# Attention's block products as chains, and PSUM banks of three kinds

## The chip, the cores and the metric

The kernel runs on one core of a Trainium2 chip. Its engines are TensorE (PE, with its weight loads shown as PEld), VectorE (DVE), ScalarE (ACT), GpSimd (POOL) and SyncE (SP), which issues most transfers. PE writes its results to PSUM, which has eight banks; one bank holds 512 float32 values in each of 128 partitions. DVE and ACT read and write PSUM too. The metric is the device time of one execution in microseconds, the median of several runs.

## What is computed

A decoder trunk of two layers on 512 positions with 1024 channels, float32 throughout. Layer 0 mixes by attention, layer 1 by causal pooling; a SwiGLU FFN of width 2816 follows each, every sub-layer starts with an RMS norm, and a last norm ends the trunk.

```python
for i in range(DEPTH):
    if i % 2 == 0:
        x = x + dilated_attention_mixer(rmsnorm(x, attn_norm[j]), w_qkv[j], w_attn_out[j])
    else:
        x = x + pooling_mixer(rmsnorm(x, pool_norm[j]), w_pool_in[j], w_pool_group[j], pool_scale[j])
    x = x + swiglu_ffn(rmsnorm(x, ffn_norm[i]), w_ffn_gate_up[i], w_ffn_down[i])
return rmsnorm(x, final_norm)
```

Attention has three groups of eight heads. In each, a query sees a causal window with a stride (windows 128, 512 and 2048, strides 1, 4 and 16) and a bias that falls with distance; the three outputs of a head slot are merged by their softmax denominators.

## The kernel before, in words

**Products in three passes.** Activations lie with channels on partitions and the 512 positions along the free axis. Each float32 operand is split in a high and a low part (`split`: an ACT copy gives `whi`, a DVE subtraction, L97, gives `wlo`), and each product is three matmuls: high by high, high by low, low by high. A plain product (`Product`, L272 to L275) has 24 matmuls of 512 columns.

**Block products.** Most weight products are done as seven block products instead of eight, in the Winograd form of Strassen's scheme: a 1024x512 piece of weights is a 2 by 2 of blocks, the activations are halves of 256 columns, and the block products are called "11", "21", "1", "3", "2", "22" and "4". Each is `mult` (L389 to L391): up to twelve matmuls of 256 columns into half a bank. The weights come in the parts b, s, m and l, two block products each except the last.

There are two ways to put the seven together before the change:

- `chain` in the FFN. Partial sums stay in PSUM. Four half-width values c, a, d, e each take a bank of their own (tags `sum`, `ps`, `seed`, `seed`). The order is: "11" into c; ACT copies c to d (L463); "1" into a, read by `share`; "2" onto c; ACT copies c to e (L471); "21" onto d, read by `left`; "3" onto c, read by `high`; "22" onto e, read by `right`; "4" onto c, read by `low`. There are 17 gate/up chains in each layer (`strassen_pair`, whose readers are L1065 to L1072: two DVE subtractions, and ACT copies and Silu) and 12 `down` chains in each layer (L1078 to L1087, whose readers are DVE additions to x; `share` has two, L1080 and L1081): 34 and 24.
- `seven` in attention, for q and k of heads 2 to 7 (18 of them) and for v of group 0 (3). It takes four banks, lets PE fill p26, p73 and p45 in both halves, and adds up on DVE (L430, L436 or L438, L443, L444), with one ACT copy at the start (L417). With `blocks` the result is written in another order of positions, by small strided pieces.

`values12` (v of groups 1 and 2, for heads 1, 3, 5 and 7) does its seven block products with the roles of weights and activations exchanged, each into a whole bank.

**Between the products.** After each block product `step` or `behind` is called. It calls `pump`, which issues at most one piece of weight preparation (loads through SP and POOL, splits on ACT and DVE) for products to come, and in attention also some work of other heads: `scores0`, `scores12`, `merge` (whose small matmuls L682 need `far` from DVE, L678), `turn0`, `turn12` (transposes), `output`. That work takes PSUM banks as well.

**Banks.** PSUM tiles are asked for by tag: `ps` 3 banks, `seed` 3, `sum` 2. Until the end of attention, a request without a tag goes through all eight in a fixed ring; later, products without a chain alternate between `ps` and `seed` (`full`), and everything else takes `ps`.

**What sets the order.** The source is traced from top to bottom, without loops at run time. The framework then fixes the order of each engine's instructions at compile time: it goes through them by an estimate of their durations, and each engine gets the earliest instruction in the source that is expected to be ready. Where the next one is expected to wait, a later one is put ahead of it. On the chip that order no longer changes. The framework places the waits too: an instruction waits for those before it in the source, on other engines, that touch the same data; in PSUM it keeps accesses of different engines to one bank in source order, whichever columns they touch. A tile's bank is handed to a new tile once all readers of the old one are done.

**PSUM sums.** In the program, a matmul with the flag `start` begins its sum anew, and does so for all places of its bank; one without it overwrites a place that hasn't been written since, and adds to one that has.

Of the kernel before, what the change touches and what calls it, by code (L numbers as in the profile page):

```python
# [15 lines left out]
P = 128  # L16
S = 512
# [34 lines left out]
def trunk(ctx: ExitStack, tc: tile.TileContext, xT, norms, w_first, w_qk, w_qkp, w_v0, w_v0p, w_v12, w_out, w_pair, w_down, w_down0, w_down1, w_down2, w_pin, w_pgrp,  # L52
# [15 lines left out]

    turn = {"ring": 0, "full": 0}
# [311 lines left out]
    def in_place(t, a=slice(0, 2)):  # L381
        return t[:, a.start * H2:a.stop * H2]
# [15 lines left out]
    def seven(T, one, two, scratch, after={}, blocks=False):  # L398


        unit, = units.popleft()
        into, left, right = by_block if blocks else in_place, slice(0, 1), slice(1, 2)

        def again(v):
            return v.unsqueeze(1).to_broadcast([P, 2, H2])

        p1, p26, p45, p73 = ps(), ps(), ps(), ps()

        def behind(i):
            pump()  # L410
            for f in after.get(i, ()):
                f()

        w = part(unit, "b")
        mult(p1[:, :H2], w, 0, T, "11")
        first, sums = scratch("first"), scratch("sums")
        nc.scalar.copy(first[:, :H2], p1[:, :H2])  # L417
        behind(0)
        mult(p26[:, :H2], w, 1, T, "21")
        w.done()  # L420
        behind(1)
        w = part(unit, "s")
        mult(p45[:, H2:], w, 0, T, "1")
        behind(2)
        mult(p73[:, :H2], w, 1, T, "3")
        w.done()
        behind(3)
        w = part(unit, "m")
        mult(p26[:, H2:], w, 0, T, "2")
        nc.vector.tensor_add(into(one), p26, again(first[:, :H2]))  # L430
        behind(4)
        mult(p73[:, H2:], w, 1, T, "22")
        w.done()
        if blocks:
            for a in (left, right):
                nc.vector.tensor_add(in_place(sums, a), in_place(p73, a), into(one, right))  # L436
        else:
            nc.vector.tensor_add(sums, p73, again(one[:, H2:]))  # L438
        behind(5)
        w = part(unit, "l")  # L440
        mult(p45[:, :H2], w, 0, T, "4")
        w.done()
        nc.vector.tensor_sub(into(two), p45, again(sums[:, :H2]))  # L443
        mark.append(nc.vector.tensor_sub(into(one, right), sums[:, H2:], p45[:, H2:]))  # L444
        behind(6)

    def chain(T, share, left, right, low, high, behind=None):


        unit, = units.popleft()  # L450
        n = unit.q // P
        c, a, d, e = (ps(tag)[:, :H2] for tag in ("sum", "ps", "seed", "seed"))
        turns = iter(range(7))

        def step():
            pump()
            i = next(turns)
            if behind:
                behind(i)

        wb = part(unit, "b")
        mult(c, wb, 0, T, "11", n=n)
        nc.scalar.copy(d, c)  # L463
# [7 lines left out]
        nc.scalar.copy(e, c)  # L471
# [12 lines left out]
        step()  # L484
        wl = part(unit, "l")
        mult(c, wl, 0, T, "4", True, n=n)
        wl.done()
        low(c)
        step()

    def normed(layer, k, row, h, t, flip=False):

# [7 lines left out]
        nc.vector.tensor_sub(t[:, H2:S], t[:, :H2], h[:, 3 * H2:])  # L500
        if flip:
            nc.vector.scalar_tensor_tensor(t[:, 3 * H2:], t[:, H2:S], -1.0, h[:, S:3 * H2],
                                           op0=OP.mult, op1=OP.subtract)
        else:
            nc.vector.tensor_add(t[:, 3 * H2:], t[:, H2:S], h[:, S:3 * H2])

    def halves_of(hi, lo):
        return [tuple(v[:, a * H2:(a + 1) * H2] for v in (hi, lo)) for a in range(2)]


# [4 lines left out]
    with tc.tile_pool(name="opool", bufs=1) as opool:  # L515
        early = opool.tile([P, HEADS, S], F32R, tag="o", name="early")
        with tc.tile_pool(name="apool", bufs=1) as apool:
# [15 lines left out]
            def values12(after={}):  # L533
# [5 lines left out]
                def product(name, half, key):  # L539
                    p = ps()  # L540
                    for a in range(2):
                        for k in range(K2):
# [3 lines left out]
                            o = both(p)[:, a]  # L546
                            nc.tensor.matmul(o, mh, wh, start=k == 0, stop=False)
                            nc.tensor.matmul(o, mh, wl, start=False, stop=False)
                            nc.tensor.matmul(o, ml, wh, start=False, stop=k == K2 - 1)
                        pump()  # L550
# [306 lines left out]
            for h in range(1, HEADS):  # L857
                for g in range(3):
# [6 lines left out]
                    else:  # L865
                        for c in range(2):
                            QKV[h, g, c] = apool.tile([P, S], F32, name=f"qk{g}{c}")
                        seven(T, QKV[h, g, 0], QKV[h, g, 1], scratch, between(h, g), g == 0)
                if h == 1:
# [8 lines left out]
                if h % 2 == 0:  # L878
                    VT[:] = [apool.tile([P, S], F32, tag=tag, name="vt") for tag in ("row", "o0")]
                    seven(T, *VT, scratch, {0: [later(scores12, h)]}, True)  # L880
                elif h < HEADS - 1:
# [24 lines left out]

            turn["ring"] = None
            for m in range(KC):
# [10 lines left out]
    with tc.tile_pool(name="fpool", bufs=1) as fpool:  # L919
# [16 lines left out]
        def ffn(layer, nxt, lead, row, wk):  # L936
# [98 lines left out]
            def prepare(k):  # L1035


                h, t = wide(("hp", k), "hp"), wide(("tp", k), "tp")
                normed(op, k, row, h, t, True)
                hq, b22 = h.rearrange("p (a b c) -> p a b c", a=2, b=2), h[:, 3 * H2:]  # L1040
# [320 lines left out]
```

## Time and profile before

| what | us |
|---|---|
| median of 3 runs | 1256.29 |
| lowest and highest | 1254.66, 1256.69 |
| the profiled execution, its own time | 1255.83 |
| its span, first to last instruction | 1254.1 |
| attention, first part with plain products | 0 to 100 |
| attention, block products | 100 to 440 |
| end of attention, output product | 440 to 510 |
| FFN of layer 0 | 510 to 854 |
| pooling | 854 to 913 |
| FFN of layer 1 | 913 to 1236 |
| last norm | 1236 to 1254 |

The lower rows are times from the start of the span. In a busy share, PE needs care: matmuls are pipelined, and the recorded length of one (0.28 us at 256 columns) is more than twice the distance to the next (0.12 us). A row of the timeline gives start and length, so the distance of starts shows a stall that a busy share hides. In a row of the waits, the numbers are total time, times and the longest.

### The profile page before, as it was taken

Reading aid. Unit: us, or ns where it says so; the run is one execution under the profiler, and the core shown is the slowest. Engines: PE = TensorE matmul, PEld = TensorE weight load, DVE = VectorE, ACT = ScalarE, POOL = GpSimd, SP = SyncE. Lnnn points to the kernel's source line nnn. Section 1 sums busy time; section 2 is a strip of 40 time slices with the busy share of each in tenths; the row PEclk is TensorE's granted clock in tenths of the full one; section 3 lists DMA queues with packets and bytes.
Section 4 is the critical chain, followed back from the end, with each engine's and each line's share of the span. In section 5 each row is a group of like instructions: output and inputs, shape, how many; then the busy total and the mean of one; then the engine's idle time right before and its main releaser. Section 6 shows DMA issues by size and latency. Waiting matters only on the chain. (4 is left out here: it accounts for less than half of the span.)

```text
span 1254.1 us, 23222 instructions
## 1 busy us (share of the span) xinstructions
PE 1237.9 (99%) x9060; PEld 1172.9 (94%) x9060; DVE 1012.5 (81%) x1687; ACT 680.2 (54%) x1171; POOL 157.4 (13%) x147
## 2 busy tenths in 40 slices
PE   9999999999999999999999999999999999999996
PEld 7889999999999998889999999988789999999996
DVE  7987788878778847798777878798999877888875
ACT  6445554445455544456456557563456646656652
POOL 1011111102111010101111111000310111111100
PEclk9999999999999999999999999999999999999998
DMA  8436566655756444437776786653145777677742
GB/s 292 107 86 173 130 158 142 162 131 156 179 135 152 127 150 132 109 85 187 186 187 165 175 202 169 153 179 118 51 118 124 176 179 183 157 201 189 172 109 68
DMA packets 76719, 189.91 MB, mean 151 GB/s; under 512 B 7600, under 2 KB 15936, under 8 KB 76608
## 3 DMA queue, kind: packets, MB, share of 16 engines
q1 hardware_dynamic: 51120, 141.74, 35.5%
q0 software_dynamic: 24336, 45.63, 22.4%
q8 instruction: 71, 1.16, 0.4%
q10 hardware_dynamic: 1152, 1.05, 0.3%
q14 instruction: 40, 0.33, 0.1%
HBM read 186.29 MB, written 2.10 MB: 150 GB/s over the span
## 5 line engine op out<-in xcount | busy, mean ns | idle before, releaser
L96 ACT ACTIVATE whi<-raw 128x1024 fp32r<-128x1024 f32 (+2 forms) x315 | 318.8, 1016 | 252.6 <-PE seed L390 78.6
L97 DVE TENSOR_TENSOR wlo<-raw,whi 128x1024 fp32r<-128x1024 f32 (+2 forms) x315 | 366.4, 1166 | 107.0 <-ACT whi L96 106.2
L158 POOL DMA_DIRECT2D raw<-w_pair x34 | 41.1, 1209 | 312.0 <-DMA raw<-w_pair 52.6
L389 PE MATMUL sum<-tt,whi 128*128 128x256 f32 x272 | 76.9, 283 | 1.2 <-ACT seed L471 0.8
L390 PE MATMUL sum<-tt,whi 128*128 128x256 f32 x272 | 76.6, 281 | 0.0
L391 PE MATMUL sum<-tt,wlo 128*128 128x256 f32 x272 | 76.4, 281 | 0.0
L96 ACT ACTIVATE halfhi<-rawhalf 128x512 fp32r<-128x512 f32 (+1 forms) x87 | 53.2, 612 | 20.0 <-PE sum L390 12.7
L173 DVE TENSOR_TENSOR raw<-raw 128x512 f32<-128x512 f32 (+1 forms) x87 | 57.5, 661 | 2.5 <-issue 2.4
L174 DVE TENSOR_TENSOR raw<-raw 128x512 f32<-128x512 f32 (+1 forms) x87 | 57.5, 661 | 0.2
L97 DVE TENSOR_TENSOR halflo<-rawhalf,halfhi 128x512 fp32r<-128x512 f32 (+1 forms) x87 | 57.4, 661 | 0.0
L158 POOL DMA_DIRECT2D raw<-w_down x24 | 28.9, 1206 | 214.1 <-DMA raw<-w_down 70.8
L389 PEld LDWEIGHTS sum<-tt,whi 128*128 128x128 f32 x272 | 51.3, 189 | 1.6 <-ACT seed L471 1.0
L471 ACT COPY seed<-sum 128x256 f32<-128x256 f32 x58 | 20.8, 359 | 57.9 <-PE sum L391 57.8
L390 PEld LDWEIGHTS sum<-tt,whi 128*128 128x128 f32 x272 | 51.2, 188 | 0.0
L391 PEld LDWEIGHTS sum<-tt,wlo 128*128 128x128 f32 x272 | 51.2, 188 | 0.0
L389 PE MATMUL sum<-hz,whi 128*128 128x256 f32 x160 | 45.4, 284 | 0.5 <-ACT seed L471 0.3
L390 PE MATMUL sum<-hz,whi 128*128 128x256 f32 x160 | 45.2, 283 | 0.0
L390 PE MATMUL seed<-hy,whi 128*128 128x256 f32 x160 | 45.2, 282 | 0.0
L391 PE MATMUL seed<-hy,wlo 128*128 128x256 f32 x160 | 45.1, 282 | 0.0
L391 PE MATMUL sum<-hz,wlo 128*128 128x256 f32 x160 | 45.1, 282 | 0.0
L389 PE MATMUL seed<-hy,whi 128*128 128x256 f32 x160 | 45.0, 281 | 0.0
L158 POOL DMA_DIRECT2D raw<-w_qkp x18 | 22.0, 1222 | 165.6 <-DMA raw<-w_qkp 100.1
(608 smaller groups left out, 4625.0 us busy)
## 6 DMA issues: line engine op xcount, KB each, us to landing
raw<-w_pair SPq DMA_DIRECT2D x78, 512.0 KB, 4.7
raw<-w_qkp SPq DMA_DIRECT2D x36, 512.0 KB, 4.4
raw<-w_pair POOLq DMA_DIRECT2D x34, 512.0 KB, 7.8
raw<-w_down SPq DMA_DIRECT2D x32, 384.0 KB, 4.2
raw<-w_v SPq DMA_DIRECT2D x18, 512.0 KB, 4.1
raw<-w_qkp POOLq DMA_DIRECT2D x18, 512.0 KB, 7.2
rawhalf<-w_pair SPq DMA_DIRECT2D x34, 256.0 KB, 4.6
raw<-w_down SPq DMA_DIRECT2D x16, 512.0 KB, 4.6
```

Of the source, the lines that this page charges most:

```text
L96: nc.scalar.activation(hi, v, AF.Copy)
L97: nc.vector.tensor_tensor(lo, v, hi.bitcast(F32), op=OP.subtract)
L158: nc.gpsimd.dma_start(b.rearrange("p (a c) -> p a c", a=2), self.src[:, None, 3 * q:].to_broadcast([P, 2, q]), accum_op=OP.add)
L173: nc.vector.tensor_add(a[:, :q], a[:, :q], b[:, :q])
L174: nc.vector.tensor_add(a[:, q:2 * q], a[:, q:2 * q], a[:, :q])
L389: nc.tensor.matmul(dst, w.t[0][:, c], th, start=k == 0 and not onto, stop=False, skip_group_check=onto)
L390: nc.tensor.matmul(dst, w.t[0][:, c], tl, start=False, stop=False, skip_group_check=onto)
L391: nc.tensor.matmul(dst, w.t[1][:, c], th, start=False, stop=k == n - 1, skip_group_check=onto)
L471: nc.scalar.copy(e, c)
```

## The change

The seven block products of attention are done by `chain` as well, and the banks are dealt out anew. `chain` now takes two banks where it took four: c and a are the halves of one `sum` bank, d and e the halves of one `seed` bank. `ps` has four banks, `seed` two, `sum` two; `ps` is for all work other than products, `full` goes through `seed`, `sum`, `ps` in turn, throughout the kernel.

Since two values share a bank, only the first matmul into it carries `start`: "1" goes onto a without it, and in `values12` ("folded values") the second half no longer has a `start` of its own. The idle matmuls at the beginning write both halves of the `seed` banks.

For `chain` to give the signs that attention needs, `normed` always makes the last quarter with the sign that the FFN had, so `low` in `seven` copies with a factor of -1, and the last subtraction of `values12` becomes an operation with the sign turned.

```diff
-RING = ("ps", "seed", "sum", "ps", "seed", "sum", "ps", "seed")
-BANKS = {"ps": 3, "seed": 3, "sum": 2}
+RING = ("seed", "sum", "ps")
+BANKS = {"ps": 4, "seed": 2, "sum": 2}
...
-    def ps(tag=None):
-
-        if tag is None:
-            if turn["ring"] is None:
-                tag = "ps"
-            else:
-                tag = RING[turn["ring"] % len(RING)]
-                turn["ring"] += 1
+    def ps(tag="ps"):
         return psum.tile([P, S], F32, tag=tag, name=tag, bufs=BANKS[tag])
 
     def full():
 
-        if turn["ring"] is not None:
-            return ps()
         turn["full"] += 1
-        return ps(("ps", "seed")[turn["full"] % 2])
+        return ps(RING[turn["full"] % len(RING)])
...
+    def halves_of(*t):
+        parts = [tuple(v[:, a * H2:(a + 1) * H2] for v in t) for a in range(2)]
+        return parts if len(t) > 1 else [v for v, in parts]
...
     def chain(T, share, left, right, low, high, behind=None):
...
-        c, a, d, e = (ps(tag)[:, :H2] for tag in ("sum", "ps", "seed", "seed"))
+        (c, a), (d, e) = (halves_of(ps(tag)) for tag in ("sum", "seed"))
...
         ws = part(unit, "s")
-        mult(a, ws, 0, T, "1", n=n)
+        mult(a, ws, 0, T, "1", True, n=n)
         share(a)
...
+    def seven(T, one, two, half, after={}, blocks=False):
+
+
+        into, left, right = by_block if blocks else in_place, slice(0, 1), slice(1, 2)
+
+        def behind(i):
+            for f in after.get(i, ()):
+                f()
+
+        chain(T, lambda p: nc.scalar.copy(half, p),
+              lambda p: nc.scalar.copy(into(one, left), p),
+              lambda p: mark.append(nc.vector.tensor_sub(into(one, right), p, half)),
+              lambda p: nc.scalar.activation(into(two, left), p, AF.Copy, scale=-1.0),
+              lambda p: nc.vector.tensor_sub(into(two, right), half, p), behind)
...
-    def normed(layer, k, row, h, t, flip=False):
+    def normed(layer, k, row, h, t):
...
                 def product(name, half, key):
-                    p = ps()
+                    p = full()
...
-                            nc.tensor.matmul(o, mh, wh, start=k == 0, stop=False)
+                            nc.tensor.matmul(o, mh, wh, start=k == a == 0, stop=False, skip_group_check=a > 0)
...
-                mark.append(nc.vector.tensor_sub(quarter(0, 1), both(m4), both(u3)))
+                mark.append(nc.vector.scalar_tensor_tensor(quarter(0, 1), both(m4), -1.0, both(u3), op0=OP.mult, op1=OP.subtract))
...
-            spare = ps()
-            for i in range(WARM):
-                nc.tensor.matmul(spare[:, :H2], idle[:, :P], idle, start=True, stop=True)
+            for i in range(WARM // 2):
+                for half, p in enumerate(halves_of(ps("seed"))):
+                    nc.tensor.matmul(p, idle[:, :P], idle, start=half == 0, stop=True, skip_group_check=half > 0)
```

The old `seven`, with its four banks and its sums on DVE, goes.

More of the change, by code (lines that the diff above doesn't have):

```diff
@@ L396, in part @@
         return unit.w[name]
[L398 to L445, printed above, removed]
+    def halves_of(*t):
+        parts = [tuple(v[:, a * H2:(a + 1) * H2] for v in t) for a in range(2)]
+        return parts if len(t) > 1 else [v for v, in parts]
     def chain(T, share, left, right, low, high, behind=None):
@@ L500, in normed @@
         nc.vector.tensor_sub(t[:, H2:S], t[:, :H2], h[:, 3 * H2:])
[L501 to L508, printed above, removed]
+        nc.vector.scalar_tensor_tensor(t[:, 3 * H2:], t[:, H2:S], -1.0, h[:, S:3 * H2], op0=OP.mult, op1=OP.subtract)
     def in_a_row(t):
@@ L546, in product @@
                             o = both(p)[:, a]
[L547 to L549 removed]
+                            nc.tensor.matmul(o, mh, wh, start=k == a == 0, stop=False, skip_group_check=a > 0)
+                            nc.tensor.matmul(o, mh, wl, start=False, stop=False, skip_group_check=a > 0)
+                            nc.tensor.matmul(o, ml, wh, start=False, stop=k == K2 - 1, skip_group_check=a > 0)
                         pump()
@@ L867, in trunk @@
                             QKV[h, g, c] = apool.tile([P, S], F32, name=f"qk{g}{c}")
-                        seven(T, QKV[h, g, 0], QKV[h, g, 1], scratch, between(h, g), g == 0)
+                        seven(T, QKV[h, g, 0], QKV[h, g, 1], scratch("half")[:, :H2], between(h, g), g == 0)
                 if h == 1:
@@ L879, in trunk @@
                     VT[:] = [apool.tile([P, S], F32, tag=tag, name="vt") for tag in ("row", "o0")]
-                    seven(T, *VT, scratch, {0: [later(scores12, h)]}, True)
+                    seven(T, *VT, scratch("half")[:, :H2], {0: [later(scores12, h)]}, True)
                 elif h < HEADS - 1:
@@ L1038, in prepare @@
                 h, t = wide(("hp", k), "hp"), wide(("tp", k), "tp")
-                normed(op, k, row, h, t, True)
+                normed(op, k, row, h, t)
                 hq, b22 = h.rearrange("p (a b c) -> p a b c", a=2, b=2), h[:, 3 * H2:]
```

3 lines of the change are left out of this document (1 added, 2 removed).

## The prediction

> **What bounds the kernel now.** I read the page first, for the engine that is never free:
>
> ```profile
> PE 1237.9 (99%) x9060; PEld 1172.9 (94%) x9060; DVE 1012.5 (81%) x1687; ACT 680.2 (54%) x1171; POOL 157.4 (13%) x147
> ```
>
> PE sets the time, and the change leaves every matmul in place (the six idle ones at the start too). So it can win only where PE stands still, and lose only where it makes PE stand still. Next, by stage (the columns are window, PE, PEld, DVE, ACT, POOL busy, granted clock, DMA share, GB/s): block attention, the first FFN, the end.
>
> ```profile
> 100.00:440.00 340.00, 337.86 (x2818) 336.33 (x2818) 272.88 (x429) 174.41 (x311) 49.44 (x50) 1.00 0.60 150
> ...
> 510.00:854.00 344.00, 341.91 (x2578) 326.72 (x2577) 288.98 (x485) 204.52 (x348) 36.79 (x31) 1.00 0.64 164
> ...
> 1236.00:1254.00 18.00, 8.15 (x52) 7.28 (x51) 9.23 (x26) 2.70 (x7) 2.92 (x4) 0.70 0.36 118
> ```
>
> Block attention has 2.1 us without PE in 340, the first FFN 2.1 in 344. DVE is 80% busy in attention (272.88 of 340) and ACT 51%, but neither is what PE waits for. PE's own waits say what is:
>
> ```profile
> PE ps L682 <- DVE far L678: 2.1, 3, 0.8
> ...
> PE sum L389 <- ACT seed L471: 1.1, 2, 0.8
> PE sum L389 <- ACT seed L463: 0.6, 2, 0.4
> ```
>
> and the waits of all engines show who follows whom:
>
> ```profile
> ACT whi L96 <- PE seed L390: 78.6, 113, 3.4
> ```
>
> Weight splits wait for PE to free a buffer, so weights are ahead of PE. The 58 FFN chains, whose copies are L463 and L471, cost PE 1.7 us in four waits: today's chain is almost free of waits because each of its four values has a bank of its own, and PE writes another bank while ACT or DVE reads.
>
> **What the change takes away.** In attention 21 products (18 for q/k, 3 for v) become chains. Two rows of the DVE groups, and one of ACT:
>
> ```profile
> L430 DVE TENSOR_TENSOR qk<-seed,first 128x512 f32<-128x512 f32 x8 | 5.5, 684 | 0.0
> ...
> L444 DVE TENSOR_TENSOR qk<-sums,sum 128x256 f32<-128x256 f32 x5 | 2.1, 412 | 0.0
> ```
>
> ```profile
> L96 ACT ACTIVATE whi<-raw 128x1024 fp32r<-128x1024 f32 x83 | 87.6, 1059 | 112.7 <-PE seed L390 25.7 <-PE ps L390 22.3 <-DVE raw L174 22.0
> ```
>
> An old product has three 128x512 DVE operations (about 0.68 each, more where they write by block) and one 128x256 (0.41): 2.46 us. A new one has two 128x256: 0.82. DVE loses at least 1.64 x 21 = 34 us. ACT goes from one 128x256 copy to five; at the 0.36 us of such a copy (quoted below, L463) that is 4 x 0.36 x 21 = 30 us more. In the attention stage DVE would fall to about 70% and ACT rise to 60%. PE hides both, so I cost them at nothing. What a lighter DVE can give back is the wait of L682 for `far`: 2.1 us. I take all of it, bounds 0 and 2.1. Start flags, the sign in `values12`, the flipped quarter in `normed` and the turn of `full` through eight banks keep their instruction counts and sizes: nothing. The small attention work gets four banks to itself; its reads are whole banks as before: nothing.
>
> **What it adds: waits.** c and a become halves of one bank, d and e halves of another. The framework orders accesses of different engines to a bank, not to its columns (section on the kernel). So three matmul groups, free today, must wait for the reader of the neighbouring half: "1" for the copy c to d (L463), "2" for the reader of a (`share`), "21" for the copy c to e (L471). "3" waits for L471 today as well. "22" now also waits for the reader of d, behind the group "3", and "4" for the reader of c, behind "22", as today. Behind a waiting matmul stands all of PE.
>
> No row of before shows such a wait, so I price it from where the readers end now. First a gate/up chain, PE and then ACT (start, length):
>
> ```profile
> 564.97 0.28 PE L389 MATMUL ps<-tt,whi 128*128 128x256 f32 x1
> ```
>
> ```profile
> 565.17 0.36 ACT L463 COPY seed<-sum 128x256 f32<-128x256 f32 x1 [0.34 <-PE sum L391]
> ```
>
> Group "1" starts at 564.97, the copy ends at 565.53: it would be held 0.56 us. Ten microseconds on, groups "2" and "21" of the next chain, and their readers:
>
> ```profile
> 576.35 0.28 PE L389 MATMUL sum<-tt,whi 128*128 128x256 f32 x1
> ...
> 577.78 0.28 PE L389 MATMUL seed<-tb,whi 128*128 128x256 f32 x1
> ```
>
> ```profile
> 576.61 0.37 ACT L1069 COPY half<-ps 128x256 f32<-128x256 f32 x1 [0.52 <-PE ps L391]
> 577.54 0.42 ACT L96 ACTIVATE hx<-t 128x256 fp32r<-128x256 f32 x1 [0.56 <-DVE t L989]
> 578.03 0.36 ACT L471 COPY seed<-sum 128x256 f32<-128x256 f32 x1
> ```
>
> "2" would be held to 576.98, 0.63 us; "21" to 578.39, 0.61 us. In `down` the reader of a is two DVE operations:
>
> ```profile
> 606.60 0.42 DVE L1080 TENSOR_TENSOR x<-x,ps 128x256 f32<-128x256 f32 x1
> 606.94 0.41 DVE L1081 TENSOR_TENSOR x<-x,ps 128x256 f32<-128x256 f32 x1
> ```
>
> ```profile
> 606.40 0.28 PE L389 MATMUL sum<-hz,whi 128*128 128x256 f32 x1
> ```
>
> They end at 607.35: 0.95 us. A held matmul also starts late after its release, and the next one later still; a wait of today that went unhidden shows how much:
>
> ```profile
> 561.54 0.42 DVE L1072 TENSOR_TENSOR up<-sum,half 128x256 f32<-128x256 f32 x1
> ```
>
> ```profile
> 561.72 0.28 PE L391 MATMUL seed<-tn,wlo 128*128 128x256 f32 x1
> 562.01 0.39 PE L389 MATMUL sum<-tt,halfhi 128*128 128x256 f32 x1
> 562.24 0.28 PE L390 MATMUL sum<-tt,halfhi 128*128 128x256 f32 x1
> ```
>
> DVE ends at 561.96, the matmul starts 0.05 later, and the next one 0.23 behind it where 0.12 is usual: 0.16 per wait. Unfilled, a gate/up chain would lose 0.56 + 0.63 + 0.61 + 3 x 0.16 = 2.28 us, a `down` chain 0.56 + 0.95 + 0.61 + 0.48 = 2.60. With 34 gate/up, 24 `down` and 21 attention chains (these at 2.28): 77.5 + 62.4 + 47.9 = 188 us. That is the upper end; the lower is nothing.
>
> The Trainium skill, "PSUM — Partial Sum Buffer", section "PSUM bank collisions raise a hardware error", speaks against this change: two engines on one bank at once collide though their columns differ, so accesses are to be kept apart by bank. No run here shows a collision. By that rule the sum is the one with waits; by columns it would be the one without.
>
> **What fills the waits.** The order of each engine is made at compile time, and PE is given later matmuls where the order expects it to wait. One case of before:
>
> ```profile
> 707.81 0.28 PE L391 MATMUL seed<-hy,wlo 128*128 128x256 f32 x1
> 707.93 0.28 PE L389 MATMUL sum<-hx,whi 128*128 128x256 f32 x1
> 708.13 0.38 PE L389 MATMUL sum<-hu,halfhi 128*128 128x256 f32 x1
> 708.36 0.28 PE L390 MATMUL sum<-hu,halfhi 128*128 128x256 f32 x1
> ```
>
> The `hx` matmul is the first of the next chain, put ahead of this chain's "4" (`hu`). The filling isn't exact: `hu` starts 0.20 us after it, not 0.12, and its successor 0.23 after that: 0.08 + 0.11 = 0.19 us lost. A worse one, with products of `a` as filling and a late L471:
>
> ```profile
> 829.52 0.40 PE L272 MATMUL ps<-a,whi 128*128 128x512 f32 x1
> 829.76 0.40 PE L273 MATMUL ps<-a,whi 128*128 128x512 f32 x1
> 830.47 0.38 PE L389 MATMUL sum<-hz,whi 128*128 128x256 f32 x1 [0.31 <-ACT seed L471]
> 830.69 0.28 PE L390 MATMUL sum<-hz,whi 128*128 128x256 f32 x1
> ```
>
> It lost 0.71 - 0.24 (from one 512-wide matmul to the next) = 0.47, and 0.22 - 0.12 = 0.10: 0.57 us.
>
> In the changed kernel the filling is the next chain's "11": twelve matmuls, 1.43 us (576.35 to 577.78 above is such a group), in the second `sum` bank, and its weights are ready early (the ACT row above). About six of them fill one wait, so the second and the third wait of a chain use them up; then "11" and its copy are already done when the next chain begins, and its first wait is gone. Two waits per chain remain, each filled but not exactly: 2 x 79 = 158. I take 0.19 us each, the row nearest to a regular filled wait: 30 us, bounds 0 and 158 x 0.57 = 90.
>
> **Sum.** Against the profiled execution's own 1255.83 us (span 1254.1 and 1.7 around it; 0.5 under the median of 1256.29): 1255.8 - 2.1 + 30 = 1284 us, slower by 2.2%.
>
> **Rivals.**
> *All waits filled* (not slower). The price falls to nothing if the order puts one matmul more than needed into each wait, which decides at about 0.2 us per wait: then only the 2.1 us of L682 count, 1253.7 us, up to 1258 if the later start of 0.03 us remains per wait. For it: four waits in 58 chains today. Against: the 0.19 and the 0.57 above.
> *No waits* (the change does not do what I say): if accesses are ordered by columns, nothing is added, 1253.7 us. Against it: the framework's order by bank.
> *Nothing to fill with.* If the next chain's operands or weights come too late, 1255.8 - 2.1 + 188 = 1442 us. Against it: ACT's 78.6 us of waiting for PE.
> *ACT late in attention.* At 60% ACT's readers may stand behind a split of 1.06 us (L96 above). If that holds for two waits in each of 21 chains, 42 x 1.06 = 45 us more: 1328. For it: scores, transposes and splits share ACT there. Against: in the FFN stage ACT is 59% busy (204.52 of 344) and its copies still start when PE is done.
> *The clock falls.* The granted clock is 1.00 in both long stages and 0.70 in the last window, where PE is busy less than half. If the small gaps brought it to 0.9 over the chains (79 of about 9.9 us, 782 us), 782 / 0.9 - 782 = 87 us more than the forecast: 1371. The Trainium skill's "TensorE: Matmul & The Clock Gate", section "A second HAM failure mode: psum-queue depth-cycling", has such a fall from small idle times at changes of bank; this trace has 99% PE busy and no fall, so it has not been put to the test.
>
> **How the numbers follow.** Forecast 0.55, all filled 0.20, no waits 0.05, nothing to fill with 0.07, ACT late 0.10, clock 0.03. A measurement of this kernel tells 0.2%, 2.5 us, from no change, so below 1253.8 is faster: I put 0.09 of the 0.25 of the first two rivals there and 0.16 within; all else, 0.75, is slower. The range runs from 1253 (no price) to 1253.7 + 90 = 1344, rounded to 1345, and leaves out the unfilled and the clock case and a little below. The forecast's own range is 1262 (a later start of 0.05 on 158 waits) to 1345.
>
> **What would show it.** Right: in the FFN, where PE has 2.1 us of gaps now, matmuls of the next chain's "11" (`sum<-tb`) between groups of the chain before, and waits of PE `sum` and `seed` matmuls on L463, L471, `share` and their kin, 0.1 to 0.3 us each, both FFN stages longer by about 11 us (29 chains x 0.38) and attention by about 6. DVE about 34 us less busy, ACT 30 more, L682's wait gone. Wrong: chains in source order with no new waits (no order by bank), waits of 0.7 us (no filling), a granted clock under 1.00 in the long stages, or a gain in attention greater than 2 us.

## The result, and the profile after

The median of six runs is **1328.88 us** (1327.17 to 1330.64), beside 1256.59 us for the kernel before (six runs, 1254.66 to 1258.60): ratio 1.0574, 95% interval 1.0563 to 1.0586, so 72 us slower. The forecast was 1284. The profiled execution took 1327.17 us, its span is 1325.4. One run of e14_all_dve below took 4010.12 us and is left out of its median; all other runs of one kernel lie within 0.6% of each other.

First the page's line of busy times, of the kernel after:

```profile
PE 1282.7 (97%) x9060; PEld 1183.3 (89%) x9060; DVE 976.5 (74%) x1636; ACT 708.4 (53%) x1255; POOL 158.5 (12%) x147
```

PE has its 9060 matmuls as before, DVE is 36.0 us less busy, ACT 28.2 us more. PE's share fell from 99% to 97%, although its busy time rose by 44.8 us: a matmul's end is modelled, so one that starts late counts as longer. The loss is therefore read from the length of stages and from starts of matmuls. The stages are cut at the first matmul of each norm's sum (`ps<-ones`). Attention, FFN 0 and FFN 1, by windows of the trace (window, length, then PE, PEld, DVE, ACT, POOL busy, granted clock, DMA share, GB/s), first before:

```profile
27.60:507.50 479.90, 477.57 (x3550) 455.95 (x3548) 369.53 (x582) 237.18 (x420) 64.34 (x67) 1.00 0.55 141
507.50:850.70 343.20, 341.11 (x2574) 326.03 (x2573) 288.45 (x484) 204.54 (x349) 37.02 (x30) 1.00 0.64 164
...
909.60:1236.80 327.20, 326.98 (x2531) 316.41 (x2530) 271.36 (x463) 191.74 (x333) 36.97 (x30) 1.00 0.62 154
```

and after:

```profile
27.90:531.50 503.60, 491.46 (x3551) 460.90 (x3549) 331.04 (x531) 266.11 (x504) 64.28 (x67) 0.99 0.52 135
531.50:898.20 366.70, 356.30 (x2575) 329.36 (x2573) 289.45 (x484) 204.62 (x349) 37.03 (x30) 1.00 0.61 153
...
957.40:1310.30 352.90, 343.50 (x2532) 319.94 (x2531) 272.93 (x463) 191.09 (x333) 36.98 (x30) 1.00 0.59 143
```

Attention grew by 23.7 us, the FFNs by 23.5 and 25.7; all the rest got 1.6 shorter. The FFN's own source differs only in the banks of its chains and of its plain products and, with them, in the flag `start` of "1". PE's waits after, for matmuls:

```profile
PE sum L380 <- ACT seed L409: 7.6, 7, 3.1
PE seed L380 <- ACT seed L417: 5.5, 19, 0.4
PE sum L500 <- ACT qk L449: 4.8, 1, 4.8
PE sum L380 <- DVE x L1038: 4.0, 8, 1.0
```

and for weight loads, which stand in the same order:

```profile
PEld seed L380 <- ACT seed L417: 21.7, 69, 0.6
PEld sum L380 <- ACT seed L409: 11.0, 15, 3.3
PEld sum L380 <- ACT up L1023: 6.2, 14, 0.8
```

L682's wait for `far` is gone. New is L417, the copy of c to e, for which "21" or its weight load now waits in nearly every chain (69 of 79), and the readers of a neighbouring half or of a bank that is handed on.

This is one gate/up chain in FFN 0, PE's starts in the timeline of the kernel after (`tb` on `sum`: "11" of a **later** chain; `tt` "2"; `tb` on `seed` "21"; `tn` "22"):

```profile
689.45 0.28 PE L382 MATMUL sum<-tb,wlo 128*128 128x256 f32 x1
689.57 0.28 PE L380 MATMUL sum<-tb,whi 128*128 128x256 f32 x1
689.84 0.39 PE L380 MATMUL sum<-tt,whi 128*128 128x256 f32 x1
690.07 0.28 PE L381 MATMUL sum<-tt,whi 128*128 128x256 f32 x1
...
691.74 0.28 PE L381 MATMUL sum<-tb,whi 128*128 128x256 f32 x1
692.04 0.39 PE L380 MATMUL seed<-tb,whi 128*128 128x256 f32 x1
692.26 0.28 PE L381 MATMUL seed<-tb,whi 128*128 128x256 f32 x1
...
694.86 0.28 PE L382 MATMUL sum<-tt,wlo 128*128 128x256 f32 x1
695.02 0.38 PE L380 MATMUL seed<-tn,whi 128*128 128x256 f32 x1
695.25 0.28 PE L381 MATMUL seed<-tn,whi 128*128 128x256 f32 x1
...
698.32 0.28 PE L382 MATMUL sum<-tb,wlo 128*128 128x256 f32 x1
698.60 0.39 PE L380 MATMUL sum<-tb,whi 128*128 128x256 f32 x1
698.82 0.28 PE L381 MATMUL sum<-tb,whi 128*128 128x256 f32 x1
```

and these are the readers on ACT that it waits for:

```profile
689.42 0.37 ACT L1021 COPY half<-sum 128x256 f32<-128x256 f32 x1 [0.52 <-PE sum L382]
...
691.63 0.36 ACT L417 COPY seed<-sum 128x256 f32<-128x256 f32 x1 [0.86 <-PE sum L382]
...
694.60 0.37 ACT L1022 ACTIVATE gt<-seed 128x256 f32<-128x256 f32 x1
...
698.17 0.38 ACT L1023 COPY up<-sum 128x256 f32<-128x256 f32 x1
```

The usual distance of two starts is 0.12 us. Each of the four groups starts 0.05 us after its reader's end (L1021 ends at 689.79, L417 at 691.99, L1022 at 694.97, L1023 at 698.55), and its second matmul follows after 0.22 or 0.23. Lost are 0.15 + 0.11 at "2", 0.18 + 0.10 at "21", 0.04 + 0.11 at "22", 0.16 + 0.10 at the put-ahead "11": 0.95 us in this stretch. The filling of "2" and of "21" is four matmuls each (689.22 to 689.57 and 691.38 to 691.74); the four up to 698.32 complete the next chain's "11", and the one at 698.60 begins "11" of the chain behind it, in the bank that this chain leaves.

### The profile page after: what moved, and what is told of

It reads as the page before. It is cut to its first block, busy times and chain, and to the rows that moved or that the text cites. A ratio compares the mean times of both kernels' runs of the same rounds, so it can differ in the third digit from the quotient of the medians.

```text
span 1325.4 us, 23199 instructions
## 1 busy us (share of the span) xinstructions
PE 1282.7 (97%) x9060; PEld 1183.3 (89%) x9060; DVE 976.5 (74%) x1636; ACT 708.4 (53%) x1255; POOL 158.5 (12%) x147
## 4 chain that ended last, share of the span: by engine, by line
PE 76%; DVE 9%; issue 7%; ACT 5%; DMA 2%; POOL 1%; POOLq 0%; ACTq 0%; SPq 0%; DVEq 0%
PE sum L380 13%; PE sum L381 11%; PE sum L382 11%; PE seed L380 6%; PE seed L381 5%; PE seed L382 4%; DVE wlo L88 2%; PE ps L264 2%; PE ps L263 2%; PE ps L266 2%; ACT whi L87 2%; PE sum L266 2%; PE sum L263 2%; PE sum L264 2%; PE seed L263 2%
## 5 line engine op out<-in xcount | busy, mean ns | idle before, releaser
L380 PE MATMUL sum<-tt,whi 128*128 128x256 f32 x408 | 118.8, 291 | 0.0
L381 PE MATMUL sum<-tt,whi 128*128 128x256 f32 x408 | 114.7, 281 | 0.0
L382 PE MATMUL sum<-tt,wlo 128*128 128x256 f32 x408 | 114.6, 281 | 0.0
L417 ACT COPY seed<-sum 128x256 f32<-128x256 f32 x79 | 28.2, 358 | 106.3 <-PE sum L382 106.1
L380 PEld LDWEIGHTS sum<-tt,whi 128*128 128x128 f32 x408 | 76.8, 188 | 6.3 <-ACT half L1021 5.5
L381 PEld LDWEIGHTS sum<-tt,whi 128*128 128x128 f32 x408 | 76.9, 188 | 0.0
L382 PEld LDWEIGHTS sum<-tt,wlo 128*128 128x128 f32 x408 | 76.8, 188 | 0.0
L380 PE MATMUL sum<-hx,whi 128*128 128x256 f32 x160 | 46.8, 293 | 10.3 <-ACT seed L409 4.5
L380 PE MATMUL seed<-h,whi 128*128 128x256 f32 x168 | 50.9, 303 | 1.3
L380 PE MATMUL seed<-hy,whi 128*128 128x256 f32 x160 | 47.5, 297 | 1.9 <-ACT seed L417 1.8
L382 PE MATMUL seed<-h,wlo 128*128 128x256 f32 x168 | 47.4, 282 | 0.0
L381 PE MATMUL seed<-h,whi 128*128 128x256 f32 x168 | 47.3, 282 | 0.0
L380 PE MATMUL sum<-hz,whi 128*128 128x256 f32 x160 | 45.9, 287 | 0.4 <-DVE x L1033 0.4
L380 PE MATMUL seed<-tb,whi 128*128 128x256 f32 x136 | 41.8, 307 | 4.5 <-ACT seed L417 3.7
```

Source lines behind the costliest of these rows:

```text
L380: nc.tensor.matmul(dst, w.t[0][:, c], th, start=k == 0 and not onto, stop=False, skip_group_check=onto)
L381: nc.tensor.matmul(dst, w.t[0][:, c], tl, start=False, stop=False, skip_group_check=onto)
L382: nc.tensor.matmul(dst, w.t[1][:, c], th, start=False, stop=k == n - 1, skip_group_check=onto)
```

## The experiments

The theory of the forecast (A): halves that share a bank make waits at "1", "2" and "21", which the next chain's "11" fills only in part. Its rivals, each told again where it is tested: the bank kinds for everything else, the chain as such in attention, and ACT, which carries more there. All ratios are to the kernel before, timed beside them. The table has the lengths of the stages (cut as above), us:

```
kernel           median   ratio [95%]               attention  FFN 0   FFN 1
before           1256.59                            479.9      343.2   327.2
after            1328.88  1.0574 [1.0563, 1.0586]   503.6      366.7   352.9
e1_ffn_share     1304.24  1.0377 [1.0362, 1.0393]   479.9      366.0   353.3
e2_own_banks     1270.89  1.0118 [1.0101, 1.0136]   494.8      342.1   327.8
e3_share_ca      1306.76  1.0397 [1.0376, 1.0418]   499.0      359.2   344.0
e4_share_de      1294.77  1.0302 [1.0268, 1.0335]   498.6      351.6   335.8
e5_no_fill       1401.84  1.1151 [1.1126, 1.1176]   501.1      404.3   391.1
e6_fill_six      1313.05  1.0448 [1.0431, 1.0465]   504.1      358.2   345.7
e7_own_dve       1272.96  1.0123 [1.0106, 1.0140]   495.7      343.1   327.6
e8_sum_three     1318.21  1.0486 [1.0460, 1.0512]   501.9      363.1   350.0
e9_held          1253.59  0.9976 [0.9967, 0.9986]   477.0      344.3   327.0
e10_chain_ring   1271.64  1.0119 [1.0100, 1.0139]   492.7      343.0   329.0
e11_early        1265.85  1.0078 [1.0061, 1.0094]   483.8      345.8   330.7
e12_order        1254.37  0.9980 [0.9969, 0.9991]   477.5      343.5   327.1
e13_de_dve       1268.77  1.0098 [1.0082, 1.0115]   490.7      342.4   329.0
e14_all_dve      1272.56  1.0116 [1.0093, 1.0140]   494.9      345.7   327.2
```

### The shared halves, alone and taken away

**e1_ffn_share**: before, with nothing but the shared halves (all the kernel's chains are in the FFN).

```diff
-        c, a, d, e = (ps(tag)[:, :H2] for tag in ("sum", "ps", "seed", "seed"))
+        (c, a), (d, e) = ((t[:, :H2], t[:, H2:]) for t in (ps("sum"), ps("seed")))
...
-        mult(a, ws, 0, T, "1", n=n)
+        mult(a, ws, 0, T, "1", True, n=n)
```

> Only the sharing of banks is put into the kernel before: c and a are halves of one sum bank, d and e of one seed bank, and "1" goes onto a without a start. Bank counts, the ring, the products of attention and all else are those of before. Theory A (the waits that come from halves in one bank cost the time, filled with later matmuls but not exactly): both FFN stages get longer as in the changed kernel, by about 24 us each, attention stays within 1 us: 1300 to 1310 us. Rival B (two seed banks instead of three and the new turn of products cost it): within 3 us of before. Rival C (the load moved to ACT in attention costs a third of it) says nothing of the FFN and expects no change in attention here.

**e2_own_banks**: after, with the old line for c, a, d, e and the old numbers of banks (`ps` 3, `seed` 3, `sum` 2).

> The changed kernel, but each of the four values of a chain has a bank of its own again (c sum, a ps, d and e seed), with three ps, three seed and two sum banks; attention's block products stay chains, and products still go through seed, sum, ps in turn. Theory A: all stages come back, attention too, 1250 to 1258 us. Rival C (five ACT copies in place of one, and the DVE work gone from attention): attention stays 15 to 24 us longer than before, 1270 to 1280 us. Rival B: the turn of products through all banks is still there, so a part stays.

The windows of the trace of e1_ffn_share, attention and FFN 0:

```profile
28.20:508.20 480.00, 477.67 (x3551) 456.00 (x3549) 369.87 (x582) 237.17 (x420) 64.28 (x67) 1.00 0.54 141
508.20:874.20 366.00, 356.44 (x2574) 329.74 (x2573) 289.55 (x484) 204.33 (x349) 37.03 (x30) 1.00 0.62 154
```

and of e2_own_banks, attention, FFN 0 and FFN 1:

```profile
27.90:522.70 494.80, 483.99 (x3549) 459.31 (x3548) 332.68 (x531) 265.28 (x504) 65.20 (x67) 0.99 0.53 137
522.70:864.80 342.10, 341.16 (x2573) 326.12 (x2572) 288.41 (x484) 205.02 (x349) 37.03 (x30) 1.00 0.64 165
924.00:1251.80 327.80, 327.29 (x2531) 316.45 (x2530) 271.56 (x463) 191.28 (x333) 36.98 (x30) 1.00 0.62 154
```

The FFN follows the halves alone: with them it has the length of after, without them that of before, whatever the other banks are. In attention they make 503.6 - 494.8 = 8.8 us, 0.42 per chain; the other 14.9 us of attention stay when each value has its own bank. That is a second cause. So e1 came out as A expected, and e2 did not: its total lies in the range of rival C, which says only that attention does not come back.

**e3_share_ca** and **e4_share_de**: after, with only c and a, or only d and e, in one bank; the other two values have banks of their own.

```diff
-        (c, a), (d, e) = (halves_of(ps(tag)) for tag in ("sum", "seed"))
+        c, a = halves_of(ps("sum"))
+        d, e = (ps("seed")[:, :H2] for i in range(2))
```

> The changed kernel, but only c and a share a bank; d and e have their own (three seed, three ps, two sum banks). Theory A: the waits at "1" and "2" and the stalls of the next chain's "11" stay, those at "21" and "22" go. In the changed kernel's trace the first three lose 43 us together and the last two 34, so 1280 to 1300 us. If only the total number of banks counted, this would be near before.

> The changed kernel, but only d and e share a bank; c and a have their own (four ps, two seed, two sum banks). Theory A: the waits at "21" and "22" stay, those at "1" and "2" go: 34 us by the changed kernel's trace, 1275 to 1290 us. Together with the run that shares c and a alone the two losses should add up to the 72 us of the change, within 15 us; less if the next chain's "11", which fills all waits, suffices when there are fewer of them.

Both totals lie above the ranges expected, which left out those 14.9 us. Each kernel has two runs; those of e4 lie 6.8 us apart, and its stages are those of the faster. In the FFN they add up: 16.0 + 8.4 = 24.4 in FFN 0 (after: 23.5), 16.8 + 8.6 = 25.4 in FFN 1 (after: 25.7). c with a costs twice what d with e does.

### The filling

**e5_no_fill**: after, with a chain's "11" ordered behind the last matmul of the chain before, so that it can't be put ahead.

```diff
-        mult(c, wb, 0, T, "11", n=n)
+        with tc.issue_after(ended[-1].ins) if ended else nullcontext():
+            mult(c, wb, 0, T, "11", n=n)
...
-        mult(c, wl, 0, T, "4", True, n=n)
+        ended.append(mult(c, wl, 0, T, "4", True, n=n))
```

> The changed kernel, with one more rule of order at compile time: the matmuls of a chain's "11" come behind the last matmul of the chain before, so that they can't fill its waits. Instructions and banks are the same. If later matmuls fill most of the new waits (theory A), the three waits of a chain now show in full, 2.3 us a gate/up chain and 2.6 us a down chain: about 410 us for each FFN stage where the changed kernel has 367 and 353 (395 for the second), 1400 to 1440 us in all. If the waits are as short as they are for another reason, the time stays at 1329 us.

FFN 0 and FFN 1 of e5_no_fill, by windows:

```profile
529.90:934.10 404.20, 361.85 (x2573) 330.09 (x2572) 289.59 (x484) 206.26 (x349) 37.03 (x30) 1.00 0.55 139
993.40:1384.50 391.10, 349.66 (x2531) 320.81 (x2530) 273.08 (x463) 193.29 (x333) 36.98 (x30) 1.00 0.53 129
```

Unfilled, the waits cost 61.0 + 63.9 = 124.9 us over 58 chains, 2.15 us each. As the kernel after is made, they cost 49.2, 0.85 each: the filling takes away three fifths. In attention the same edit costs nothing (501.1 us beside 503.6): there the next chain's "11" is not what fills the waits.

**e6_fill_six**: after, with the filling written into the source of the FFN's chains: six matmuls of the next "11" after "1", the rest after "2".

```diff
         share(a)
         step()
+        ahead(range(2))
...
         nc.scalar.copy(e, c)
         step()
+        ahead(range(2, n))
```

> The changed kernel, with the filling written out in the source for chains that follow each other in the FFN: six matmuls of the next chain's "11" stand behind "1", the rest of "11" behind "2". In the changed kernel's trace three or four matmuls stand there, and the group behind still loses about 0.25 us. Theory A with an order that fills too little: six cover 0.71 us of a hold of 0.6 to 0.65, so the loss at "2" and "21" falls below 0.12 us each and the stalls of "11" go; an FFN stage falls from 367 and 353 us by 10 to 18 us each, 1295 to 1310 us in all. If the loss comes with any wait, however long it is filled, the stages stay within 4 us.

**e8_sum_three**: after, with three `sum` banks and three `ps`, so that a put-ahead "11" need not wait for the bank of the chain that has just ended.

```diff
-BANKS = {"ps": 4, "seed": 2, "sum": 2}
+BANKS = {"ps": 3, "seed": 2, "sum": 3}
```

> The changed kernel with three sum banks instead of two, and three ps instead of four. The next chain's "11", put ahead as filling, waits in the changed kernel for the last reader of the bank it takes over (14 us of lost time on "11" in the FFN). Theory A: with a third bank those stalls go, 5 to 7 us per FFN stage, 1312 to 1320 us; the waits at "2" and "21" stay. Rival B, that the number of banks matters more than the sharing, expects over 20 us.

Six fillers win 8.5 + 7.2 us in the FFNs and 15.8 in the median, less than I expected: 33.5 us of the FFN's 49.2 remain. Where they remain is seen when every distance of two starts beyond the usual one is added up by the group that starts late: in gate/up chains it falls from 31.2 to 15.5 us ("21" from 13.2 to 4.5, while "22" keeps its 4), in `down` chains it stays (26.1 and 25.7). In 16 of the 24 `down` chains a group has nine matmuls, not twelve, so behind six only three are left for "21". A third `sum` bank wins 10.7 us in the median, and 3.6 + 2.9 in the FFNs, where I had expected 5 to 7 each: "11" no longer waits for the bank, but late starts of "1" behind the copy L409 grow from 6.8 to 12.6 us.

### Attention's own 14.9 us

**e7_own_dve**: e2_own_banks with the readers `left` and `low` of attention on DVE.

> The kernel in which each value of a chain has its own bank (1270.9 us), but in attention two of the five ACT copies of a block product (left and low) are done by DVE. If attention's 15 us come from ACT being late (three stalls of 1.7 to 4.0 us behind L409 and L449), they shrink to less than 7 us: attention 480 to 487 us, 1256 to 1263 us in all. If chains as such are slower in attention, it stays within 3 us of 1271.

Nothing is gained (1272.96 beside 1270.89; attention 495.7 in place of 480 to 487).

**e9_held**: before, with the weight slots of `seven` given back to the plan later.

```diff
         mult(p26[:, :H2], w, 1, T, "21")
-        w.done()
...
         mult(p73[:, :H2], w, 1, T, "3")
-        w.done()
+        wb.done()
...
         mult(p26[:, H2:], w, 0, T, "2")
+        ws.done()
```

> The kernel before with one edit: in the attention's block product (seven, L398 to L444) the slot of weight block b is given back to the splitting plan after the fourth product and not after the second, that of block s after the fifth and not after the fourth, as the chain has to do it. Theory H (the attention's own +14.9 us, which banks of their own did not take away, comes from weight blocks that are held longer, so that the split of the next ones, then the raw buffer, then the load of the next weights come later): attention from 479.9 us to 487 to 495, total 1264 to 1272. Theory K (it comes from the banks of the other products, 3 or 4 of one kind in place of a ring over 8) and theory R (it comes from the chain's own copies and readers): attention within 2 us of 479.9, total 1255 to 1259.

**e10_chain_ring**: e2_own_banks with before's ring over eight banks for all that is no chain. Here a d or e can come into a bank of which the product before wrote only some places, and by the rule for `start` "21" or "22" then begins anew there instead of adding to the copy, so this kernel leaves a part of some sums out. That is worked out from the flags, not shown by a run; PE, DVE and ACT have as many instructions as in e2_own_banks.

> The kernel after with four banks for the values of each chain (as in e2_own_banks), and with the bank ring of the kernel before for all other products: attention's block products are chains, nothing else of the bank plan is changed. Theory K (bank kinds): attention falls from 494.8 to within 4 us of 479.9, total 1256 to 1261. Theories H and R (the chain itself, by its held weight blocks or by its copies and readers): attention 490 to 498, total 1266 to 1274.

**e11_early**: e2_own_banks with "21" ahead of "2". The edit reaches the gate/up chains too, which pass a `behind` as well; they lose 3.7 and 2.9 us by it.

```diff
+        if not behind:
+            wm = second()
         mult(d, wb, 1, T, "21", True, n=n)
         wb.done()
         left(d)
         step()
+        if behind:
+            wm = second()
```

> e2_own_banks with another order of products in the attention's chains alone: 11, 1, 21, 2, 3, 22, 4 in place of 11, 1, 2, 21, 3, 22, 4. Block b of the weights is free after the third product and not after the fourth; in return 3 follows the copy of e at once, a wait of 0.56 us per chain that the next chain's matmuls may fill (21 chains). Theory H (held weight blocks): attention falls by 2 to 8 us below 494.8, total 1263 to 1269. Theories K and R: attention unchanged or up to 8 us longer, total 1270 to 1279.

**e12_order**: before, with `seven`'s products in the chain's order 11, 1, 2, 21, 3, 22, 4.

> The kernel before with one edit: the seven products of the attention's block product (seven) are issued in the chain's order 11, 1, 2, 21, 3, 22, 4 in place of 11, 21, 1, 3, 2, 22, 4. They stay in their four banks, their readers stay as they were (the sum over 21 and 2 at the same place behind the fifth product), there is no chain, no copy of c, no new wait between products; only the matmuls that read weight block b last come two products later and those of block s one product later. Theory H (PE releases the weight blocks later, so the splits, the raw buffers and the loads come later): attention from 479.9 to 488 to 495, total 1264 to 1272. Theory R (the chain's own copies and readers make the attention's 14.9 us, and e11_early helped by moving those): attention within 3 us of 479.9, total 1253 to 1260.

**e13_de_dve** and **e14_all_dve**: e2_own_banks with the copies of c on DVE; then `left` and `low` there too.

```diff
-        nc.scalar.copy(d, c)
+        copy(d, c)
...
-              lambda p: nc.vector.tensor_sub(into(two, right), half, p), behind)
+              lambda p: nc.vector.tensor_sub(into(two, right), half, p), behind, nc.vector.tensor_copy)
```

> e2_own_banks with the two copies of the attention's chains (d from c, e from c, L409 and L417) on DVE in place of ACT; the readers stay on ACT. Theory R (PE waits for copies that stand on ACT behind a weight split whose load is late: ACT waits 6.9 us for raw<-w_v at 197.98, then runs eight exponentials, and only then L449 and L409, for which PE stands): the stalls for L409 and L417 go, those for the reader L449 (3.9 and 2.6 us) stay: attention from 494.8 to 486 to 493, total 1262 to 1269. Theory V (the engine does not matter, DVE's own part of the splits puts the copies late there as well): attention 493 to 500, total 1269 to 1276.

> e13_de_dve with the two readers left and low (L447, L449) on DVE as well, so that of the attention's chains only the copy of half stays on ACT. Theory R: PE waits for ACT no longer, attention 480 to 487, total 1256 to 1263. Theory V: attention 493 to 500, total 1269 to 1276.

Bank kinds are not the cause (e10), and neither is the plan (e9) nor the chain's order by itself (e12: 477.5 us). Yet with chains that order matters: the earlier "21" of e11 brings attention from 494.8 to 483.8. The engine of the copies matters little: e7 gains nothing, e13's 490.7 lies in the range of theory R but its median is only 2.1 us under that of e2, and e14, for which R expected 480 to 487, has 494.9. PE's three long waits in attention are the same in all of them. First e2_own_banks, then e13_de_dve and e14_all_dve, where they are for DVE:

```profile
PE sum L500 <- ACT qk L449: 3.9, 1, 3.9
PE ps L607 <- ACT qk L449: 2.6, 1, 2.6
PE sum L380 <- ACT seed L409: 2.2, 4, 1.6
```

```profile
PE sum L380 <- DVE seed L409: 8.9, 3, 3.4
...
PE sum L380 <- DVE seed L409: 8.5, 3, 3.3
```

The traces say how these fit together. At one place of head 3, ACT in the kernel after:

```profile
198.58 1.06 ACT L87 ACTIVATE whi<-raw 128x1024 fp32r<-128x1024 f32 x1 [6.41 <-DMA raw<-w_v]
199.55 0.39 ACT L594 ACTIVATE s<-s,nm 128x128 f32<-128x128 f32 x1
...
201.41 0.36 ACT L449 ACTIVATE qk<-sum 128x256 f32<-128x256 f32 x1
```

and PE there:

```profile
196.74 0.28 PE L382 MATMUL sum<-h,wlo 128*128 128x256 f32 x1
201.82 0.39 PE L500 MATMUL sum<-whi,h 128*128 128x256 f32 x1 [4.80 <-ACT qk L449]
```

A weight split waits 6.41 us for a late load; behind it stand four exponentials (L594) and the reader L449, and PE stands still until that is done. In e12_order, where the products have separate banks and their readers are DVE's, ACT waits for the same kind of load as well:

```profile
193.78 1.06 ACT L96 ACTIVATE whi<-raw 128x1024 fp32r<-128x1024 f32 x1 [4.39 <-DMA raw<-w_v]
```

while PE is busy throughout:

```profile
185.00:200.00 15.00, 15.00 (x123) 14.84 (x122) 12.46 (x20) 8.04 (x17) 2.53 (x3) 1.00 0.51 123
```

In e11_early the block is free earlier and the wait is short:

```profile
193.54 1.06 ACT L87 ACTIVATE whi<-raw 128x1024 fp32r<-128x1024 f32 x1 [1.30 <-DMA raw<-w_v]
```

In e14_all_dve the copy stands on DVE, behind the other part of the split:

```profile
197.54 1.23 DVE L88 TENSOR_TENSOR wlo<-raw,whi 128x1024 fp32r<-128x1024 f32 x1 [2.88 <-ACT whi L87]
198.68 0.43 DVE L409 COPY seed<-sum 128x256 f32<-128x256 f32 x1
```

and PE waits for it there:

```profile
199.25 0.36 PE L380 MATMUL sum<-t,whi 128*128 128x256 f32 x1 [2.49 <-DVE seed L409]
```

The same stands at three places of e2_own_banks: splits at 197.98, 313.52 and 426.80 wait 6.90, 4.71 and 4.44 us for `w_v`, and PE behind them 3.9, 1.6 and 2.6 us, 8.1 in all. With 2.9 us by a fall of the clock (last section) that is 11.0 of the 14.9. In e12_order the three loads are late too (4.39, 4.52 and 3.28 us), and PE has no pause over 0.3 us in the block products. In e11_early two waits of 1.3 us are left, PE waits at most 0.7 us for a copy, the clock does not fall in that stage, and attention is 11.0 us shorter.

So it takes both: the chain's order makes a weight load late, which alone costs nothing, and the chain makes PE depend at once on a copy or a reader that stands behind the split of that weight, on whichever engine. Either engine's order is fixed, so the copy can't pass. e11 shows the one half of it, e12 the other; the 3.9 us that e11 still has over the kernel before were not traced, and that a chain whose copies are kept ahead of the splits would lose nothing was not tried.

## Why the prediction was right and wrong

**Right: the mechanism of the halves.** e1 and e2 show it alone and taken away. The waits come at "2" and "21", "1" is rid of its wait in a regular gate/up chain, the next "11" fills, DVE and ACT change by -36 and +28 (forecast -34 and +30), L682's wait goes. The unfilled price was near too: 2.28 and 2.60 forecast, a mean of 2.41 over 34 and 24 chains, 2.15 measured by e5. The rivals "no waits", "all filled" and "nothing to fill with" fall with e1 and e5.

**Wrong: "two waits per chain remain", "158 x 0.19 = 30 us".** That is the step that failed in the FFN: 0.38 us per chain forecast, 0.85 measured, 49.2 us in place of 22.0 for its 58 chains. Both factors were too small. The late starts of the kernel after, added up over both FFN stages by what ended just before (each with its restart), are 51.9 us, where the kernel before has 3.0 of the kind:

| group | behind | us |
|---|---|---|
| "21" | the copy L417 | 19.9 |
| "2" | `share` (L1021, L1033) | 9.5 |
| "11", put ahead | the last reader of the bank it takes (L1023, L1038) | 11.6 |
| "1", nearly all in `down` | the copy L409 | 6.8 |
| "22" | the reader of d (L1022) | 4.1 |

The two waits that I had priced, "2" and "21", cost 29.4 us, 0.51 per chain. "About six" matmuls per wait should have used up "11", but in the chain above the order takes four, so each filled wait ends 0.15 to 0.18 us too late and costs 0.10 more at the restart (0.26 and 0.28, not 0.19); and in most `down` chains "11" has nine matmuls, not twelve. The other 22.5 us are at places that I had passed over: "22" with the words that it waits "behind the group 3", the bank of the put-ahead "11", and the first wait, which is not gone where "11" is not done early enough. In `down` a reader can also stand behind a split on DVE: L1038 starts at 741.12 behind one of 0.95 us, and "11" starts 1.19 us late. In attention the halves cost 0.42 per chain (e2), close to the forecast, but by luck: the filling that I had counted on does not matter there (e5: 501.1 us without it).

**Wrong: "PE hides both, so I cost them at nothing".** Attention as chains costs 14.9 us before any bank is shared. The cover was PE's own work: `seven` has four banks under way and goes on while a reader is late. A chain's next product needs the copy of c, or a bank whose reader is late, and PE's order is fixed, so the cover ends there: 4.8 us in the one wait shown (L500). The rival "ACT late in attention" gave 1328, almost the measured time, but by luck: readers did stand behind splits, as it said, but at a few places (three in e2_own_banks), not in 42 waits; its 45 us were all to come from attention, which lost 23.7 us, and the larger part of the loss is in the FFN.

**The sum.** 27.2 us too little in the FFNs (49.2 - 22.0), 17.8 too little in attention (23.7 - 5.9, the forecast of 21 x 0.38 less 2.1): 1284 + 45 = 1329. The 1.6 us that the rest got shorter bring this to the 1327 of the profiled execution.

**The clock.** As a rival, at 0.9 over all chains, it did not come: 1.00 in both FFN stages. But it has a small part in attention, 3.4 us; see the last section.

**What is faster than both.** The kernel before with `seven`'s weight slots held longer in the plan (e9, 0.9976, interval 0.9967 to 0.9986) or with its products in the chain's order (e12, 0.9980, 0.9969 to 0.9991). In both, L682's wait is gone from PE's waits; that this is all of the gain wasn't tried apart.

## What to carry to other kernels

Before putting two accumulators in one bank, list for every group of matmuls the reader of the neighbouring half and the reader that hands the bank on: each is a wait on PE, and one that the compile-time order fills still cost about 0.25 us here, 0.85 us per chain of seven products. The whole banks that became free by it won nothing that shows here. And if partial sums are kept in PSUM, ask what stands ahead of the copies in their engine's fixed order; a late load that hurt nobody becomes PE's wait.

## What the hardware showed besides

A pause of PE costs a second time. The page's row of 40 slices has a 9 for the granted clock nearly throughout, but windows of 1 us behind the pause at 196.74 to 201.82 show it, in the kernel after:

```profile
202.00:203.00 1.00, 1.00 (x7) 1.00 (x8) 0.96 (x3) 0.60 (x2) 0.00 (x0) 0.60 0.00 0
203.00:204.00 1.00, 1.00 (x6) 1.00 (x6) 0.43 (x1) 0.00 (x0) 0.00 (x0) 0.50 0.00 0
204.00:205.00 1.00, 1.00 (x7) 1.00 (x6) 0.00 (x0) 0.00 (x0) 0.00 (x0) 0.50 0.46 104
205.00:206.00 1.00, 1.00 (x8) 1.00 (x8) 0.00 (x0) 0.38 (x1) 0.00 (x0) 0.70 0.54 156
```

Half the clock for about 3.4 us: 0.4 + 0.5 + 0.5 + 0.3 = 1.7 us lost. The pause that ends at 436.13 is followed by a second such fall (0.86, 0.50, 0.50, 0.50 and 0.94 in the windows from 437 to 442), so the clock has about 3.4 of attention's 23.7 us. In e2_own_banks there is one fall, which begins in the pause that ends at 201.22 and lasts until about 207; PE loses 0.50 x 5.8 = 2.9 us by it:

```profile
201.20:207.00 5.80, 5.78 (x27) 5.78 (x28) 1.69 (x3) 1.42 (x4) 0.00 (x0) 0.50 0.15 45
```

The Trainium skill, "TensorE: Matmul & The Clock Gate", section "What's actually happening", has the clock halved after an idle window of about 3.4 us and restored after a busy one of that length; the length of the fall agrees. But in e14_all_dve a pause of 2.65 us (196.48 to 199.25, less the usual 0.12) was followed by 0.50 from 201 to 204, so a pause shorter than the window can be enough; in e13_de_dve one of 2.9 us at 310 was not followed by a fall. In e8_sum_three even two short pauses close together, 0.93 us up to 433.21 and 1.14 us up to 434.47, were followed by one (0.57 over 434 to 438). What decides it is open.
